# Two hybrid decoder layers on one core: the mixers' small VectorE operations merged or moved to GpSimd and ScalarE

## The chip, the core and the metric

The kernel runs on one core of a Trainium2 chip. The metric is the time of one execution in microseconds of the device, from the start of the program to its end; a kernel is timed several times and the median counts. The profile beside it comes from one further execution. The engines are TensorE (PE in the rows, with its weight loads as PEld), VectorE (DVE), ScalarE (ACT), GpSimd (POOL), and SyncE (SP), which issues the DMAs here.

## What is computed

Two decoder layers over 512 tokens of width 1024, in float32. Each layer is a SwiGLU feed-forward (inner width 2816), a mixer, and a second SwiGLU, each with a residual and a layer norm behind it. The mixer projects the stream once and runs three token mixers side by side: RWKV-7 (8 heads of 64), differential attention with ALiBi (4 heads), and a chunked gated DeltaNet (4 heads of 128). Their outputs go through one projection each, are weighted by sigmoid gates, summed and projected again.

```
for l in range(2):
    x = LN(a*x + 0.5*swiglu(x, ffn1))
    h = x @ mix_w_in                                   # 1024 -> 8456 columns
    ya = rwkv7(h[...])        # l2norm of keys, decay cumulated over 64 tokens, state update, group norm
    yb = diff_attention(h[...])   # softmax(q1 k1) - lam*softmax(q2 k2), rmsnorm
    yc = gated_deltanet(h[...])   # conv, l2norm of q and k, exp(G_i - G_j) inside chunks of 64, rmsnorm
    merged = sum_n sigmoid(h[gates_n]) * (y_n @ w_branch[n])
    x = LN(a*x + merged @ mix_w_out)
    x = LN(a*x + 0.5*swiglu(x, ffn2))
```

## The kernel before

Activations stand with their features on the partitions (`xTh`, `xTl`: 128 x 8 x 512, a rounded part and its remainder). Weights come in by DMA as 128x1024 tiles `wr`; ScalarE rounds each to `wh` and VectorE subtracts to `wl`, and a product is three TensorE passes (high x high, high x low, low x high). `proj` makes one tile of 128 features x 512 tokens in 24 such passes of 512 columns; these are the `pj`, `pg`, `pu` and `pgt` matmuls in the rows.

The feed-forwards are long runs of these. In the mixer (`mix`, `main`) the twelve head units of a layer come in the order `RDRDRRDGGDGG`: R is a pair of RWKV heads (`rw_pair`), D an attention head (`da_head`), G a DeltaNet head (`gdn_head`). `main` is the stream of projections; each unit is a generator that yields between its stages, and up to four units are open. `pump` decides when the next stage of a unit is written into the program: a planner (`Estimate`, lines 81 to 132) adds up a price for every instruction on its engine, and a stage is let in when its inputs are due by the planner's own TensorE time. So the planner's prices set the order in which TensorE meets projections and unit stages, and each engine then works its instructions off in order. The prices are on lines 91 to 95 and 113: 70 ns plus 0.52 or 1.04 ns for each element on VectorE, 80 ns plus an 1/1.2 ns each (94 ns more with a scalar of the tile) on ScalarE, 150 ns plus 2.1 ns each on GpSimd, but 600 ns plus 150 ns for each column of a power.

Places that the change touches:

- `rsqrt` (L258) scales and adds on VectorE, and then makes the inverse root. For one column (the layer norms) that is a power on GpSimd; for 4 or 8 columns it is 11 VectorE operations of 128x4 or 128x8, a bit trick and three Newton steps, in which each needs the one before. `rw_pair` calls it for the group norm (L1005, 8 columns, tile `gn`; then `Y` is scaled and transposed into `pyT`), `gdn_head` for the key and query norms (L1121, 8 columns, `gnrm`) and its output norm (L1211, 4 columns, `gss`), `da_head` for its output norm (L1283, 4 columns, `dss`). That is 32 calls: 16 with 8 columns, 16 with 4. The temporary tiles are `rst` and `rsy`.
- `rw_pair` cumulates the decay `G` by eight scans of 64 tokens (L822), and masks and scales its triangular matrix `L` out of PSUM by eight operations of 128x128 (L879). `L` then goes through `inverse`, which writes it to memory by DMA and reads its 16x16 blocks back as `LX`; 15 rounds of two small VectorE operations (`Tb`, `LX`) invert them.
- `gdn_head` makes, for each half of the tokens, the operands `gr` of the decay matrix by eight 128x128 operations (L1137).
- `da_head` negates a row maximum `dmx` for each of the two maps of a block (L1260) and takes the exponential right behind it (L1261).
- All 128x128 temporaries share 12 buffers (L163).

Of the kernel before, what the change touches and what calls it, by code (L numbers as in the profile page):

```python
# [134 lines left out]
class Net:  # L135
# [17 lines left out]
    def t2(self, shape=(128, 512), dt=F32, name="t2"):  # L153
        return self.t2p.tile(list(shape), dt, tag="t2", name=name)
# [5 lines left out]
        return self.smp.tile([128, n], F32, tag=name, name=name, bufs=bufs)  # L160

    def m128(self, name):
        return self.smp.tile([128, 128], F32, tag="m", name=name, bufs=12)  # L163

    def mm(self, out, lhsT, rhs, **kw):
        return self.nc.tensor.matmul(out, lhsT, rhs, **kw)
# [16 lines left out]
    def more_consts(self):  # L183
        nc, c = self.nc, self.const
        P = 128

        def tri(name, sign, base):
            m = c.tile([P, P], F32, name=name)
            nc.gpsimd.affine_select(out=m, in_=self.ones, pattern=[[-sign, P]], compare_op=ALU.is_ge,
                                    fill=0.0, base=base, channel_multiplier=sign)  # L190
            return m

        self.m_gt = tri("m_gt", 1, -1)
        self.m_le = tri("m_le", -1, 0)
        self.r_gt, self.r_le = (c.tile([P, P], F32R, name=n) for n in ("r_gt", "r_le"))
        nc.gpsimd.tensor_copy(out=self.r_gt, in_=self.m_gt)
        nc.gpsimd.tensor_copy(out=self.r_le, in_=self.m_le)
        self.r_id = c.tile([P, P], F32R, name="r_id")
        nc.gpsimd.tensor_copy(out=self.r_id, in_=self.ident)
        self.neg = c.tile([P, 2, 2, P], F32R, name="neg")  # L200
        for i, m in enumerate((self.m_gt, self.m_le)):
            for j in range(2):
                nc.gpsimd.tensor_scalar(out=self.neg[:, i, j, :], in0=m, scalar1=1e30, scalar2=-1e30, op0=ALU.mult,
                                        op1=ALU.add)

        def pair(name, src, r0):
            m = c.tile([P, P], F32, name=name)
            nc.gpsimd.tensor_copy(out=m, in_=src)
            nc.gpsimd.memset(m[r0:r0 + 64, 64 - r0:128 - r0], 0.0)
            return m  # L210

        self.b_gt = pair("b_gt", self.m_gt, 64)

        self.m3 = c.tile([P, 3, 64], F32, name="m3")
        for h in range(2):
            r = slice(64 * h, 64 * h + 64)
            for j in range(3):
                nc.gpsimd.affine_select(out=self.m3[r, j, :], in_=self.ones[r, 0:64], pattern=[[1, 64]],
                                        compare_op=ALU.is_ge, fill=0.0, base=-1 if j == 0 else 0, channel_multiplier=-1)
        self.bd = c.tile([P, P], F32, name="bd")  # L220
        nc.gpsimd.memset(self.bd, 0.0)
        nc.gpsimd.memset(self.bd[0:64, 0:64], 1.0)
        nc.gpsimd.memset(self.bd[64:128, 64:128], 1.0)
        self.r_bd = c.tile([P, P], F32R, name="r_bd")
        nc.gpsimd.tensor_copy(out=self.r_bd, in_=self.bd)

        b, nb = 16, P // 32
        self.lev = c.tile([P, P], F32, name="lev")
        nc.gpsimd.memset(self.lev, 0.0)
        v = self.lev.rearrange("p (n h b) -> p n h b", h=2, b=b)[:, :, 0, :]  # L230
        nc.gpsimd.memset(v, 1.0)
        nc.gpsimd.affine_select(out=v, in_=v, pattern=[[-2 * b, nb], [0, b]], compare_op=ALU.is_ge,
                                fill=0.0, base=-b, channel_multiplier=1)
        nc.gpsimd.affine_select(out=v, in_=v, pattern=[[2 * b, nb], [0, b]], compare_op=ALU.is_ge,
                                fill=0.0, base=2 * b - 1, channel_multiplier=-1)
        zt = self.t2(name="zt")
        nc.gpsimd.memset(zt, 0.0)
        self.xd, self.nxd = [], 0
        for _ in range(3):
            t = self.tc.dram_tile([8 * BLK], F32, name="Xd")  # L240
            nc.sync.dma_start(out=t[0:128 * 1024].rearrange("(p c) -> p c", p=128)[:, 0:512], in_=zt)
            nc.sync.dma_start(out=t[0:128 * 1024].rearrange("(p c) -> p c", p=128)[:, 512:1024], in_=zt)
            nc.sync.dma_start(out=t[128 * 1024:].rearrange("(p c) -> p c", p=128), in_=zt[:, 0:8])
            self.xd.append(t)

        self.ndist = c.tile([P, 512], F32, name="ndist")
        nc.gpsimd.iota(self.ndist, pattern=[[1, 512]], base=-384, channel_multiplier=-1,
                       allow_small_or_imprecise_dtypes=True)
        nc.gpsimd.affine_select(out=self.ndist, in_=self.ndist, pattern=[[-1, 512]], compare_op=ALU.is_ge,
                                fill=-1e30, base=384, channel_multiplier=1)  # L250
        self.mhalf = c.tile([P, 16], F32, name="mhalf")
        nc.gpsimd.memset(self.mhalf, -0.5)
# [5 lines left out]
    def rsqrt(self, out, in_, scale, eps, n):  # L258
        nc = self.nc
        nc.vector.tensor_scalar(out=out, in0=in_, scalar1=scale, scalar2=eps, op0=ALU.mult, op1=ALU.add)  # L260
        if n == 1:
            nc.gpsimd.tensor_tensor(out=out, in0=out, in1=self.mhalf[:, 0:n], op=ALU.pow)
            return

        V, y, t = nc.vector, self.sm(n, "rsy"), self.sm(n, "rst")
        V.tensor_scalar(out=t.bitcast(I32), in0=out.bitcast(I32), scalar1=1, scalar2=None, op0=ALU.logical_shift_right)
        V.tensor_scalar(out=y.bitcast(I32), in0=t.bitcast(I32), scalar1=-1, scalar2=0x5f3759df, op0=ALU.mult, op1=ALU.add)
        for i in range(3):
            V.tensor_tensor(out=t, in0=y, in1=y, op=ALU.mult)
            V.scalar_tensor_tensor(out=t, in0=t, scalar=-0.5, in1=out, op0=ALU.mult, op1=ALU.mult)  # L270
            V.scalar_tensor_tensor(out=out if i == 2 else y, in0=t, scalar=1.5, in1=y, op0=ALU.add, op1=ALU.mult)

# [521 lines left out]
    def rw_pair(self, j, r, k, v):  # L796
# [22 lines left out]
        sq = t2(name="sq")  # L819
        nc.scalar.activation(out=sq, in_=p.rearrange("p t c -> p (t c)"), func=ACTF.Square)  # L820
        G = t2(name="G")
        for c in range(8):  # L822
            s = slice(64 * c, 64 * c + 64)
            nc.vector.tensor_tensor_scan(out=G[:, s], data0=self.ones[:, 0:64], data1=lw[:, s],
                                         initial=0.0, op0=ALU.mult, op1=ALU.add)

        VU, KB = ([t2((128, 4, 128), name=n) for _ in range(2)] for n in ("VU", "KB"))
        p = self.psum((128, 4, 128), "pv2")
# [32 lines left out]
        for h in range(2):  # L861
            TT(out=c4(AR[h][:, :, 0, :])[:, :, :, 1:64], in0=c4(AR[h][:, :, 0, :])[:, :, :, 1:64],
               in1=c4(hv(E, h))[:, :, :, 0:63], op=ALU.mult)
            nc.gpsimd.tensor_tensor(out=AR[h][:, :, 1, :], in0=hv(r, h), in1=hv(E, h), op=ALU.mult)
        yield

        pb = self.psum(name="pb")
# [2 lines left out]
        bv = v  # L870
        TT(out=bv, in0=v, in1=pb, op=ALU.mult)

        Ls = [t2((128, 4, 128), name="L") for _ in range(2)]
        ps = [self.psum((128, 4, 128), "pL") for _ in range(2)]
        for tt in range(NT):
            for e in range(2):
                rs = slice(64 * e, 64 * e + 64)
                self.mm(ps[e][:, tt, :], AR[tt // 2][rs, tt % 2, 0, :], be[rs, 128 * tt:128 * tt + 128], start=True, stop=True)
        for e in range(2):  # L879
            for tt in range(NT):  # L880
                STT(out=Ls[e][:, tt, :], in0=ps[e][:, tt, :], scalar=n2[:, 2 * tt + e:2 * tt + e + 1], in1=self.b_gt,
                    op0=ALU.mult, op1=ALU.mult)
        yield
        inv = self.inverse([L.rearrange("p a b -> p (a b)") for L in Ls], False)
        next(inv)
# [216 lines left out]
    def gdn_head(self, h, k, q, v, sz):  # L1102
# [30 lines left out]
        for tp in range(2):  # L1133

            gr = [t2((128, 2, 2, 128), dt=F32R, name="gr") for _ in range(2)]
            for e in range(2):
                for q in range(2):  # L1137
                    g1 = self.g2[e][:, 2 * tp + q, h:h + 1]
                    nc.vector.tensor_scalar(out=gr[e][:, 0, q, :], in0=self.m_gt, scalar1=g1, scalar2=None, op0=ALU.mult)
                    nc.vector.tensor_scalar(out=gr[e][:, 1, q, :], in0=self.m_le, scalar1=g1, scalar2=None, op0=ALU.mult)  # L1140
            yield
            pd = self.psum((128, 2, 2, 128), "pd")
            self.mm(pd, self.r_id, self.neg, start=True, stop=False, skip_group_check=True)
            for e in range(2):
                self.mm(pd[:, 0], self.r_le, gr[e][:, 0], start=False, stop=e == 1, skip_group_check=True)
            for e in range(2):
# [92 lines left out]
    def da_head(self, h, q, k, v):  # L1239
# [7 lines left out]
        for i in range(NT):  # L1247
            n = 128 * (i + 1)
            ex = []
            sm = self.sm(2, "dsum", bufs=4)  # L1250
            for m in range(2):
                w = max(n, 256)
                p = self.psum((128, w), "psc")
                self.mm64(p, q, k, m, slice(128 * i, 128 * i + 128), slice(0, w))
                p = p[:, 0:n]
                t = t2((128, n), name="dsc")
                mx = self.sm(2, "dmx", bufs=4)
                nc.vector.tensor_tensor_reduce(out=t, in0=p, in1=self.ndist[:, 128 * (3 - i):512], scale=1.0,
                                               scalar=-3e38, op0=ALU.add, op1=ALU.max, accum_out=mx[:, 0:1])
                nc.vector.tensor_scalar(out=mx[:, 1:2], in0=mx[:, 0:1], scalar1=-slope, scalar2=None, op0=ALU.mult)  # L1260
                nc.scalar.activation(out=t, in_=t, func=ACTF.Exp, scale=slope, bias=mx[:, 1:2], accum_out=sm[:, m:m + 1])  # L1261
                ex.append(t)
            yield

            c = self.sm(2, "dc", bufs=4)
# [159 lines left out]
```

## Time and profile before

| | |
|---|---|
| timed runs | 2860.83, 2865.65, 2866.03 us; median 2865.65 us |
| profiled execution | 2866.84 us, of which the span from its first to its last instruction is 2865.0 us |
| TensorE busy | 2817.8 us (98% of the span), 15728 matmuls |
| VectorE busy | 1657.9 us (58%), 3760 instructions |
| ScalarE busy | 1015.4 us (35%), 1805 instructions |
| GpSimd busy | 157.2 us (5%), 205 instructions |
| the mixers | about 400 to 870 us and 1800 to 2340 us of the span |

Busy means that at least one instruction of the engine was under way; a matmul of 512 columns lasts 389 ns in the record although 222 of them start in 50 us of a feed-forward, so a busy TensorE need not be at its best rate. A wait is idle time of an engine, put down to the instruction that released it. The granted clock is the share of full speed that TensorE was given; it has two levels, 1.2 and 2.4 GHz, shown as 0.50 and 1.00.

### The profile page before, as it was taken

The numbers are of one execution on the slowest core, as the hardware profiler recorded it, in microseconds if no ns is written. First come the engines' busy times: TensorE is split into PE (matmuls) and PEld (weight loads), VectorE is DVE, ScalarE is ACT, GpSimd is POOL, SyncE is SP. The second block draws the span as 40 slices with busy tenths as digits, with TensorE's granted clock in tenths as the row PEclk, the third lists the DMA queues.
The fourth block names the chain that finished last, engine by engine and source line by source line (L and its number), as shares of the span: only waits on it lengthen the run. The fifth ranks groups of instructions, "written<-read, shape, count | busy, mean of one in ns | idle before, by whom it ended". The sixth has DMA issues, their size and how long they took to land. (4 is left out here: it accounts for less than half of the span.)

```text
span 2865.0 us, 40194 instructions
## 1 busy us (share of the span) xinstructions
PE 2817.8 (98%) x15728; PEld 2333.7 (81%) x15728; DVE 1657.9 (58%) x3760; ACT 1015.4 (35%) x1805; POOL 157.2 (5%) x205
## 2 busy tenths in 40 slices
PE   9999999999999999999999999999999999999998
PEld 8888887778878888888888888777788788888887
DVE  4333568788874463443643335677888745633345
ACT  3222345444543332222422223454445433322222
POOL 1000021010000010000100000210100000100001
PEclk9999999999999999999999999999999999999999
DMA  6433423222223353333533334222222234533332
GB/s 179 126 98 99 141 75 84 67 72 55 71 72 88 101 180 101 98 96 97 155 96 113 101 96 134 82 71 69 69 61 65 72 89 117 163 109 97 96 96 89
DMA packets 436350, 282.18 MB, mean 98 GB/s; under 512 B 39432, under 2 KB 391872, under 8 KB 436160
## 3 DMA queue, kind: packets, MB, share of 16 engines
q1 hardware_dynamic: 436160, 279.60, 33.5%
q8 instruction: 124, 2.03, 0.3%
q14 instruction: 66, 0.54, 0.1%
HBM read 258.31 MB, written 21.25 MB: 98 GB/s over the span
## 5 line engine op out<-in xcount | busy, mean ns | idle before, releaser
L66 DVE TENSOR_TENSOR wl<-wr,wh 128x1024 fp32r<-128x1024 f32 x406 | 500.1, 1232 | 655.7 <-ACT wh L66 652.4
L66 ACT CAST wh<-wr 128x1024 fp32r<-128x1024 f32 x406 | 427.4, 1053 | 1252.4 <-issue 550.9
L66 PE MATMUL pu<-xTh,wh 128*128 128x512 f32 x672 | 261.6, 389 | 0.0
L66 PE MATMUL pu<-xTh,wl 128*128 128x512 f32 x672 | 261.4, 389 | 0.0
L66 PE MATMUL pu<-xTl,wh 128*128 128x512 f32 x672 | 261.4, 389 | 0.0
L66 PE MATMUL oa<-wh,hl 128*128 128x512 f32 x640 | 249.0, 389 | 0.0
L66 PE MATMUL pg<-xTh,wh 128*128 128x512 f32 x640 | 249.0, 389 | 0.0
L66 PE MATMUL pg<-xTl,wh 128*128 128x512 f32 x640 | 249.0, 389 | 0.0
L66 PE MATMUL pg<-xTh,wl 128*128 128x512 f32 x640 | 249.0, 389 | 0.0
L66 PE MATMUL oa<-wh,hh 128*128 128x512 f32 x640 | 249.0, 389 | 0.0
L66 PE MATMUL oa<-wl,hh 128*128 128x512 f32 x640 | 249.0, 389 | 0.0
L66 PE MATMUL pj<-xTh,wh 128*128 128x512 f32 x560 | 229.1, 409 | 0.0
L66 PE MATMUL pj<-xTh,wl 128*128 128x512 f32 x560 | 227.7, 407 | 0.0
L66 PE MATMUL pj<-xTl,wh 128*128 128x512 f32 x560 | 225.7, 403 | 0.0
L66 DVE TENSOR_TENSOR ft<-ft,pu 128x512 f32<-128x512 f32 x84 | 57.7, 687 | 226.5 <-PE pu L66 226.4
L66 PE MATMUL pgt<-xTh,wh 128*128 128x512 f32 x384 | 153.0, 398 | 0.0
L66 PE MATMUL pgt<-xTh,wl 128*128 128x512 f32 x384 | 150.4, 392 | 0.0
L66 PE MATMUL pgt<-xTl,wh 128*128 128x512 f32 x384 | 150.3, 391 | 0.0
L66 PEld LDWEIGHTS pu<-xTh,wl 128*128 128x128 f32 x672 | 126.2, 188 | 26.2
L66 PEld LDWEIGHTS pu<-xTl,wh 128*128 128x128 f32 x672 | 126.2, 188 | 26.0
L66 PEld LDWEIGHTS pu<-xTh,wh 128*128 128x128 f32 x672 | 126.0, 188 | 26.2
L66 PEld LDWEIGHTS pg<-xTh,wh 128*128 128x128 f32 x640 | 120.2, 188 | 25.2
(397 smaller groups left out, 5295.5 us busy)
## 6 DMA issues: line engine op xcount, KB each, us to landing
wr<-in_ffn_w_in_dram SPq DMA_DIRECT2D x176, 512.0 KB
wr<-in_mix_w_in_dram SPq DMA_DIRECT2D x132, 512.0 KB
wr<-in_ffn_w_out_dram SPq DMA_DIRECT2D x88, 512.0 KB
wr<-in_mix_w_branch_dram SPq DMA_DIRECT2D x24, 512.0 KB
xres<-x SPq DMA_DIRECT2D x40, 256.0 KB
x<-xres SPq DMA_DIRECT2D x40, 256.0 KB
wr<-in_mix_w_out_dram SPq DMA_DIRECT2D x16, 512.0 KB
iX<-Xd SPq DMA_DIRECT2D x24, 256.0 KB
```

The costliest lines, as they stand in the source:

```text
L66: r = f(*args, **kw)
```

## The change

- `rsqrt` keeps its first VectorE operation and makes the inverse root by one GpSimd power for any number of columns.
- The eight scans become one of 512 columns, with a constant `seg` (ones, but zero at the start of each 64) that multiplies the running sum.
- The eight masked and scaled copies of `L` become eight ScalarE copies of the mask scaled by the norm, made one stage earlier, and two VectorE products of 128x512 with PSUM.
- The eight `gr` operations become two VectorE products of 128x512 with broadcast operands; the constant `neg` is halved and broadcast into its matmul.
- The two negations of `dmx` become one, and both exponentials stand behind both reductions.
- The buffers of the 128x128 temporaries go from 12 to 10.

```diff
     def rsqrt(self, out, in_, scale, eps, n):
         nc.vector.tensor_scalar(out=out, in0=in_, scalar1=scale, scalar2=eps, op0=ALU.mult, op1=ALU.add)
-        if n == 1:
-            nc.gpsimd.tensor_tensor(out=out, in0=out, in1=self.mhalf[:, 0:n], op=ALU.pow)
-            return
-        V, y, t = nc.vector, self.sm(n, "rsy"), self.sm(n, "rst")
-        V.tensor_scalar(out=t.bitcast(I32), in0=out.bitcast(I32), scalar1=1, scalar2=None, op0=ALU.logical_shift_right)
-        V.tensor_scalar(out=y.bitcast(I32), in0=t.bitcast(I32), scalar1=-1, scalar2=0x5f3759df, op0=ALU.mult, op1=ALU.add)
-        for i in range(3):
-            V.tensor_tensor(out=t, in0=y, in1=y, op=ALU.mult)
-            V.scalar_tensor_tensor(out=t, in0=t, scalar=-0.5, in1=out, op0=ALU.mult, op1=ALU.mult)
-            V.scalar_tensor_tensor(out=out if i == 2 else y, in0=t, scalar=1.5, in1=y, op0=ALU.add, op1=ALU.mult)
+        nc.gpsimd.tensor_tensor(out=out, in0=out, in1=self.mhalf[:, 0:n], op=ALU.pow)
...
-        for c in range(8):
-            s = slice(64 * c, 64 * c + 64)
-            nc.vector.tensor_tensor_scan(out=G[:, s], data0=self.ones[:, 0:64], data1=lw[:, s],
-                                         initial=0.0, op0=ALU.mult, op1=ALU.add)
+        nc.vector.tensor_tensor_scan(out=G, data0=self.seg, data1=lw,
+                                     initial=0.0, op0=ALU.mult, op1=ALU.add)
...
+        Ls = [t2((128, 4, 128), name="L") for _ in range(2)]
+        for e in range(2):
+            for tt in range(NT):
+                nc.scalar.activation(out=Ls[e][:, tt, :], in_=self.b_gt, func=ACTF.Copy, scale=n2[:, 2 * tt + e:2 * tt + e + 1])
         yield
...
         for e in range(2):
-            for tt in range(NT):
-                STT(out=Ls[e][:, tt, :], in0=ps[e][:, tt, :], scalar=n2[:, 2 * tt + e:2 * tt + e + 1], in1=self.b_gt,
-                    op0=ALU.mult, op1=ALU.mult)
+            TT(out=Ls[e], in0=ps[e], in1=Ls[e], op=ALU.mult)
...
             for e in range(2):
-                for q in range(2):
-                    g1 = self.g2[e][:, 2 * tp + q, h:h + 1]
-                    nc.vector.tensor_scalar(out=gr[e][:, 0, q, :], in0=self.m_gt, scalar1=g1, scalar2=None, op0=ALU.mult)
-                    nc.vector.tensor_scalar(out=gr[e][:, 1, q, :], in0=self.m_le, scalar1=g1, scalar2=None, op0=ALU.mult)
+                TT(out=gr[e], in0=self.m_2[:, :, None, :].to_broadcast([128, 2, 2, 128]),
+                   in1=self.g2[e][:, None, 2 * tp:2 * tp + 2, h:h + 1].to_broadcast([128, 2, 2, 128]), op=ALU.mult)
...
-                nc.vector.tensor_scalar(out=mx[:, 1:2], in0=mx[:, 0:1], scalar1=-slope, scalar2=None, op0=ALU.mult)
-                nc.scalar.activation(out=t, in_=t, func=ACTF.Exp, scale=slope, bias=mx[:, 1:2], accum_out=sm[:, m:m + 1])
                 ex.append(t)
+            nc.vector.tensor_scalar(out=mx[:, 2:4], in0=mx[:, 0:2], scalar1=-slope, scalar2=None, op0=ALU.mult)
+            for m, t in enumerate(ex):
+                nc.scalar.activation(out=t, in_=t, func=ACTF.Exp, scale=slope, bias=mx[:, 2 + m:3 + m],
+                                     accum_out=sm[:, m:m + 1])
```

## Rows read from the trace of the kernel before

**Rows 1.** The page: busy us of each engine, share of the span, instructions.

```profile
PE 2817.8 (98%) x15728; PEld 2333.7 (81%) x15728; DVE 1657.9 (58%) x3760; ACT 1015.4 (35%) x1805; POOL 157.2 (5%) x205
```

**Rows 2.** Mixers: stretch, length, busy PE, PEld, DVE, ACT, POOL, granted clock, DMA.

```profile
400.00:870.00 470.00, 456.21 (x3427) 369.38 (x3426) 381.99 (x1272) 230.46 (x530) 40.18 (x52) 1.00 0.27 70
1800.00:2340.00 540.00, 527.38 (x3791) 430.90 (x3791) 413.34 (x1336) 251.81 (x568) 41.14 (x55) 0.98 0.26 70
```

**Rows 3.** Waits of PE over the span: releaser, us in total, times, longest.

```profile
PE pyT L66 <- DVE Y L66: 4.5, 2, 2.5
PE ip L66 <- DVE iZ L66: 4.2, 4, 1.4
PE pG L66 <- DVE gg L66: 4.0, 2, 2.0
...
PE pb L66 <- ACT sqh L66: 1.1, 2, 0.5
PE pMV L66 <- DVE M L66: 1.0, 2, 0.5
...
PE pyT L66 <- DVE gO L66: 0.7, 2, 0.3
...
PE pyT L66 <- DVE dO L66: 0.5, 1, 0.5
```

**Rows 4.** Timeline, DVE around 552 us: start, length, instruction, idle before.

```profile
550.20 0.16 DVE L66 TENSOR_SCALAR rst<-dss 128x4 int32<-128x4 int32 x1
552.64 0.17 DVE L66 TENSOR_TENSOR Tb<-LX 64x15 f32<-64x15 f32 x1 [2.28 <-DMA LX<-Ld]
```

**Rows 5.** Timeline, PE, layer 1's longest wait for `Y`.

```profile
556.17 0.63 PE L66 MATMUL pyT<-ident,Y 128*128 128x128 f32 x4 [1.94 <-DVE Y L66]
```

**Rows 6.** Timeline, PE, layer 2's longest wait for `Y`.

```profile
1982.45 0.31 PE L66 MATMUL pyT<-ident,Y 128*128 128x128 f32 x1 [2.52 <-DVE Y L66]
```

**Rows 7.** One stretch at the lower clock, and the sum of all four; columns of rows 2.

```profile
1982.60:1986.00 3.40, 3.40 (x14) 3.01 (x14) 1.97 (x9) 1.21 (x2) 0.00 (x0) 0.50 0.00 0
sum 20.40, PE 20.40 PEld 14.96 DVE 14.77 ACT 6.45 POOL 4.03; mean PE 5.10 PEld 3.74 DVE 3.69 ACT 1.61 POOL 1.01
```

**Rows 8.** Whole span, instructions with `rst` alone: busy DVE, clock, DMA.

```profile
0.00:2865.00 2865.00, 53.15 (x352) 0.99 0.34 98
```

**Rows 9.** Timeline, DVE: first and last of eleven operations of one inverse root.

```profile
713.23 0.13 DVE L66 TENSOR_SCALAR rst<-gn 128x8 int32<-128x8 int32 x1
...
716.21 0.17 DVE L66 SCALAR_TENSOR_TENSOR gn<-rst,rsy 128x8 f32<-128x8 f32 x1
```

**Rows 10.** POOL, power of one column: count, least, median, most ns; first and last start.

```profile
L66 POOL TENSOR_TENSOR lnrs<-lnrs,mhalf x24: 547/550/1527, 359.6 to 2859.6; 128x1 f32<-128x1 f32 x24
```

**Rows 11.** Timeline, DVE and POOL around 1428 us.

```profile
1427.13 1.71 DVE L66 TENSOR_TENSOR wl<-wr,wh 128x1024 fp32r<-128x1024 f32 x1
1427.71 1.53 POOL L66 TENSOR_TENSOR lnrs<-lnrs,mhalf 128x1 f32<-128x1 f32 x1
```

**Rows 12.** DVE groups: shapes, count, busy us, mean ns, idle before.

```profile
L66 DVE TENSOR_TENSOR wl<-wr,wh 128x1024 fp32r<-128x1024 f32 x406 | 500.1, 1232 | 655.7 <-ACT wh L66 652.4 <-ACT ipt L66 1.8 <-DMA Ld<-L 0.2
...
L66 DVE SCALAR_TENSOR_TENSOR L<-pL,n,b_gt 128x128 f32<-128x128 f32 x64 | 18.3, 341 | 0.9 <-PE pL L66 0.9
...
L66 DVE TENSOR_TENSOR_SCAN G<-ones,lw 128x64 f32<-128x64 f32 x64 | 12.5, 269 | 0.4
...
L66 DVE TENSOR_SCALAR dmx<-dmx 128x1 f32<-128x1 f32 x64 | 8.6, 143 | 0.1
...
L66 DVE TENSOR_TENSOR R<-pMV,nn 128x512 f32<-128x512 f32 x8 | 5.5, 686 | 1.6 <-PE pMV L66 1.5
```

**Rows 13.** Whole span, instructions with `gr` alone: busy PE, PEld, DVE, clock, DMA.

```profile
0.00:2865.00 2865.00, 11.09 (x64) 9.81 (x64) 29.80 (x128) 0.99 0.34 98
```

**Rows 14.** ACT group: a 128x128 activation with a scalar of the tile.

```profile
L66 ACT ACTIVATE dO<-pdo,drs 128x128 f32<-128x128 f32 x32 | 11.9, 370 | 19.5 <-PE pdo L66 19.3
```

**Rows 15.** Timeline, ACT, the rounding that the `pb` matmul waits for.

```profile
476.00 0.62 ACT L66 CAST sqh<-sq 128x512 fp32r<-128x512 f32 x1 [1.41 <-DVE sq L66]
```

More of the change, by code (lines that the diff above doesn't have):

```diff
@@ L162, in m128 @@
     def m128(self, name):
-        return self.smp.tile([128, 128], F32, tag="m", name=name, bufs=12)
+        return self.smp.tile([128, 128], F32, tag="m", name=name, bufs=10)
     def mm(self, out, lhsT, rhs, **kw):
@@ L185, in more_consts, with tri @@
         P = 128
-        def tri(name, sign, base):
-            m = c.tile([P, P], F32, name=name)
+        self.m_2 = c.tile([P, 2, P], F32, name="m_2")
+        def tri(m, sign, base):
             nc.gpsimd.affine_select(out=m, in_=self.ones, pattern=[[-sign, P]], compare_op=ALU.is_ge,
@@ L191, in tri @@
             return m
-        self.m_gt = tri("m_gt", 1, -1)
-        self.m_le = tri("m_le", -1, 0)
+        self.m_gt = tri(self.m_2[:, 0, :], 1, -1)
+        self.m_le = tri(self.m_2[:, 1, :], -1, 0)
         self.r_gt, self.r_le = (c.tile([P, P], F32R, name=n) for n in ("r_gt", "r_le"))
@@ L199, in more_consts @@
         nc.gpsimd.tensor_copy(out=self.r_id, in_=self.ident)
-        self.neg = c.tile([P, 2, 2, P], F32R, name="neg")
+        self.neg = c.tile([P, 2, P], F32R, name="neg")
         for i, m in enumerate((self.m_gt, self.m_le)):
-            for j in range(2):
-                nc.gpsimd.tensor_scalar(out=self.neg[:, i, j, :], in0=m, scalar1=1e30, scalar2=-1e30, op0=ALU.mult,
-                                        op1=ALU.add)
+            nc.gpsimd.tensor_scalar(out=self.neg[:, i, :], in0=m, scalar1=1e30, scalar2=-1e30, op0=ALU.mult, op1=ALU.add)
         def pair(name, src, r0):
@@ L219, in more_consts @@
                                         compare_op=ALU.is_ge, fill=0.0, base=-1 if j == 0 else 0, channel_multiplier=-1)
+        self.seg = c.tile([P, T], F32, name="seg")
+        nc.gpsimd.memset(self.seg, 1.0)
+        nc.gpsimd.memset(self.seg.rearrange("p (c i) -> p c i", c=8)[:, :, 0:1], 0.0)
         self.bd = c.tile([P, P], F32, name="bd")
@@ L871, in rw_pair @@
         TT(out=bv, in0=v, in1=pb, op=ALU.mult)
-        Ls = [t2((128, 4, 128), name="L") for _ in range(2)]
         ps = [self.psum((128, 4, 128), "pL") for _ in range(2)]
@@ L1136, in gdn_head @@
             for e in range(2):
-                for q in range(2):
-                    g1 = self.g2[e][:, 2 * tp + q, h:h + 1]
-                    nc.vector.tensor_scalar(out=gr[e][:, 0, q, :], in0=self.m_gt, scalar1=g1, scalar2=None, op0=ALU.mult)
-                    nc.vector.tensor_scalar(out=gr[e][:, 1, q, :], in0=self.m_le, scalar1=g1, scalar2=None, op0=ALU.mult)
+                TT(out=gr[e], in0=self.m_2[:, :, None, :].to_broadcast([128, 2, 2, 128]),
+                   in1=self.g2[e][:, None, 2 * tp:2 * tp + 2, h:h + 1].to_broadcast([128, 2, 2, 128]), op=ALU.mult)
             yield
             pd = self.psum((128, 2, 2, 128), "pd")
-            self.mm(pd, self.r_id, self.neg, start=True, stop=False, skip_group_check=True)
+            self.mm(pd, self.r_id, self.neg[:, :, None, :].to_broadcast([128, 2, 2, 128]), start=True, stop=False,
+                    skip_group_check=True)
             for e in range(2):
@@ L1250, in da_head @@
             sm = self.sm(2, "dsum", bufs=4)
+            mx = self.sm(4, "dmx", bufs=4)
             for m in range(2):
@@ L1256, in da_head @@
                 t = t2((128, n), name="dsc")
-                mx = self.sm(2, "dmx", bufs=4)
                 nc.vector.tensor_tensor_reduce(out=t, in0=p, in1=self.ndist[:, 128 * (3 - i):512], scale=1.0,
-                                               scalar=-3e38, op0=ALU.add, op1=ALU.max, accum_out=mx[:, 0:1])
-                nc.vector.tensor_scalar(out=mx[:, 1:2], in0=mx[:, 0:1], scalar1=-slope, scalar2=None, op0=ALU.mult)
-                nc.scalar.activation(out=t, in_=t, func=ACTF.Exp, scale=slope, bias=mx[:, 1:2], accum_out=sm[:, m:m + 1])
+                                               scalar=-3e38, op0=ALU.add, op1=ALU.max, accum_out=mx[:, m:m + 1])
                 ex.append(t)
+            nc.vector.tensor_scalar(out=mx[:, 2:4], in0=mx[:, 0:2], scalar1=-slope, scalar2=None, op0=ALU.mult)
+            for m, t in enumerate(ex):
+                nc.scalar.activation(out=t, in_=t, func=ACTF.Exp, scale=slope, bias=mx[:, 2 + m:3 + m],
+                                     accum_out=sm[:, m:m + 1])
             yield
```

## The prediction

> **What bounds the kernel now.** The first part of the page comes first: TensorE is busy for 2817.8 of 2865.0 us, VectorE for 1657.9 [rows 1]. So 47.2 us is all that better timing can give without less matmul work, and the change takes away no matmul. The table by stretches says where to look: in the two mixers TensorE idles for 13.8 us (470.0 - 456.21) and 12.6 us (540.0 - 527.38), 26.4 us together, while VectorE is busy for 81% and 77% [rows 2]. The feed-forwards and their layer norms hold the other 20.8 us, and nothing in them changes: their one-column roots are powers already. Then the waits of TensorE: nearly all those of the mixers end on VectorE [rows 3]. The longest kind is the transpose `pyT` behind the group norm, 4.5 us in two waits. The timeline shows how it comes about: at 550.20 VectorE has made the first step of two inverse roots; the next instruction in its order belongs to the block inversion and waits 2.28 us for a DMA, and the ten steps of each root that are left come behind it, woven among the inversion's small products [rows 4]. TensorE has meanwhile stopped for 1.94 us [rows 5]; layer 2 does the same with 2.52 us [rows 6]. One more loss hangs on such stops: in layer 2's mixer the granted clock is at 0.50 (1.2 GHz) for four stretches, 20.4 us, and one of them, 3.4 us, begins at 1982.6 right behind the 2.52 us stop [rows 6, 7]. Layer 1 has the same stops and no such stretch (clock 1.00 [rows 2]), so a stop makes one possible, not certain.
>
> The profiled execution took 2866.84 us, 1.2 above the median of 2865.65; the sum below starts from 2866.84.
>
> **Inverse roots.** 32 calls lose 11 operations each, 352, which keep VectorE busy for 53.15 us [rows 8]; part of that lies over neighbours, so it is an upper figure. What counts more is the length of the chain: 713.23 to 716.38, 3.15 us, with one weight subtraction in between [rows 9], and from 550.20 past 555 where it waits for the DMA. The power that replaces it is on another engine, whose queue holds 81.3 us of work in both mixers' 1010 us [rows 2], and so cannot be caught behind that DMA wait. Its price for 4 or 8 columns stands in no row. One column takes 550 ns [rows 10]; below, all columns cost what one does, 0.55 us; above, each costs as much, 2.2 and 4.4 us. I take 1.2 and 1.8 us, the planner's own prices and nearer the lower end, since the one-column time must hold a start-up. With 1.8 the chain is shorter than the shortest one measured, and even 4.4 us is under the 5 us around 552.
>
> Contention is the point to be careful about. At 1427.71 a one-column power took 1.53 us beside a VectorE subtraction that took 1.71 [rows 11], against 0.55 and a mean of 1.23 [rows 10, 12]. So up to 1.0 us comes on top of a power, and up to 0.5 us on a VectorE operation; 32 x 0.5 = 16 us of VectorE at most.
> The Trainium skill (GPSIMD Engine Reference, section 8, Key points) says that GpSimd shares its SBUF interfaces with VectorE and contends with operations that have two SBUF inputs; that speaks against this move, and the 1.53 us agrees with it. By that rule the contention would fall on most of the 32 powers; it has its place below as the slow power.
>
> Behind the roots in the program: `Y` is scaled by VectorE in a stage of its own, so other work can stand between; in `gdn_head` (`bs`, `kws`, `nqs`) and before the scaling of `dO` and `gO` the next VectorE operation of the same stage needs the power, and if nothing stands between them VectorE idles for about as long as it worked before. There I count nothing.
>
> So: the two waits for `Y` go, 4.5 us; the wait for `dO` (the chain of its root fills the time ahead of it) 0.5; the two of `pMV` for `M`, in which steps of a root stand between, 1.0 [rows 3]. That is 6.0 us. What is late next behind `Y` is its own scaling, which needs VectorE after the DMA wait, so by 552.64 + 0.67 = 553.3; the stop begins at 556.17 - 1.94 = 554.2, so nothing is left.
>
> **The merged operations.** None stands on a path that TensorE was seen to wait for; they lighten VectorE. `gr`: 29.8 us [rows 13] against 32 products of 128x512 at 0.686 us, 22.0 [rows 12]: 7.8 back.
> The Trainium skill (VectorE: DVE Perf Modes, section The perf-mode tier table) has it the other way: a float32 tensor_scalar in SBUF at twice the rate of a tensor_tensor. By rate alone this merge would cost VectorE time, an estimate of 0.53 us for each of 16 sets from its 0.96 GHz, 8.5 us instead of the gain, and 1.5 us of relief below instead of 1.9. The rows differ from it, and they decide: the fixed part of a 128-column operation outweighs the rate.
> `L`: 18.3 against 16 x 0.686 = 11.0 [rows 12]: 7.3 back. The scans: 12.5 for 64 [rows 12]; one of 512 lies between a product's 0.69 us and eight scans' 1.57; half way, 1.1, gives 3.7 back, the ends 0 and 7. `dmx`: half of 8.6, 4.3 back. With the roots, 76 us of the 795 that VectorE is busy in the mixers [rows 2], 10%. The ten other kinds of wait that end on VectorE there, from `ip` (4.2) by `pG` (4.0) down to `pyT` for `gO` (0.7), make 18.7 us [rows 3]; a tenth of that is 1.9 us. It could be nothing, as most of them end chains that the change leaves alone, or half.
>
> **Added to ScalarE.** 64 copies of 128x128 with a scalar. The nearest row has 0.370 us [rows 14]: 23.7 us, 2.96 for each pair of RWKV heads. ScalarE is busy for 48% of the mixers [rows 2], and it idled 1.41 us before it rounded `sqh`, for which TensorE waits already [rows 3, 15]. The planner adds 2.25 us to that stage and lets the next in later, with projections in between, so I take nothing on TensorE; without cover it is 23.7 us. The rest (two buffers less, one constant read by broadcast) I take at nothing, as no wait in rows 3 is for such a buffer; if one came up, it would cost what a wait there costs, 0.3 to 2.5 us.
>
> **Sum.** 6.0 + 1.9, and the 3.4 us at half clock behind the stop of 1982, half of which is loss, 1.7: 9.6 us. 2866.84 - 9.6 = 2857.2. Against the median that is 8.4 us less, 0.3%.
>
> **Rivals.**
> (a) The gain is taken back by the new order. Prices fall on VectorE and rise on GpSimd and ScalarE, so projections and stages meet in another order everywhere in the mixers, and other waits of half a microsecond to two come up. For it: 26.4 us of waits are left to be dealt anew; against it: the planner prices the eleven operations at 74 to 78 ns, 0.85 us, and they took 3.15 [rows 9], and it is these that go, so that the plan comes nearer to what happens. About 2864 us.
> (b) The other three stretches at half clock go too, (20.4 - 3.4) / 2 = 8.5 us more [rows 7]: 2848.7. For it: layer 1 does without them. Against it: the stops before them (`pG`, `pb`) are not on the changed chains.
> (c) Slower: ScalarE, in order, does the eight copies ahead of `sqh` and of the weights' rounding. Of 2.96 us, 1.41 has cover; 1.55 x 8 = 12.4 us late: 2866.84 - 9.6 + 12.4 = 2869.6. With no cover 2866.84 - 9.6 + 23.7 = 2880.9. It decides from 9.6 / 8 = 1.2 us for each pair that reach TensorE.
> (d) The slow power: 4.4 us and 1.0 for contention, 5.4. The other six pairs show no wait for `Y` [rows 3], with chains 2.3 us over the planned 0.85 [rows 9]; over the power's planned 1.8 that makes 4.1, and 16 x 1.3 = 20.8 us: 2878.0. It decides from 4.7 us for 8 columns.
>
> **Chances.** Forecast 0.42, its own range 2853 to 2861; (a) 0.28; (b) 0.15; (c) 0.10, half of it without cover; (d) 0.05. About 0.2%, 5.7 us, is what a measurement can tell here: below 2859.9 is faster, above 2871.4 slower. Faster: 0.36 of the forecast and 0.15 of (b), 0.51. Slower: 0.05 of (c), 0.05 of (d) and 0.02 of (a), 0.12. Same: 0.37. The range goes from just under (b), 2847, to just over the covered (c), 2870.
>
> **What the changed profile would show.** Right: no `pyT` wait for `Y` over 1 us; powers of 8 columns near 1.8 us; VectorE's busy time down by 50 to 76 us; TensorE idle in the mixers near 18 us. Wrong: waits of TensorE on ScalarE for `sqh` or on `L`; powers over 4 us with VectorE idle behind them; TensorE idle at 26 us again under other names; more stretches at 0.50, which would hide the gain.

## The result, and the profile after

The changed kernel takes 2892.09 us (median of four runs, 2890.37 to 2892.33) against 2865.84 us for the kernel before on the same chip: 1.009 times as long, 95% interval 1.0073 to 1.0108. That is 26 us slower, where 8.4 us less was forecast. Its profiled execution took 2890.37 us with a span of 2888.4 us, 23.4 us more than before.

The page's first part (columns as in [rows 1]) and the mixers by windows (columns as in [rows 2]):

```profile
PE 2828.9 (98%) x15728; PEld 2341.2 (81%) x15728; DVE 1618.5 (56%) x3176; ACT 1030.8 (36%) x1869; POOL 202.8 (7%) x237
```

```profile
400.00:870.00 470.00, 450.79 (x3305) 363.58 (x3304) 352.30 (x959) 230.77 (x545) 60.05 (x66) 0.97 0.26 69
1800.00:2340.00 540.00, 518.17 (x3763) 422.24 (x3762) 398.24 (x1054) 259.36 (x601) 73.58 (x78) 0.99 0.26 69
```

VectorE is busy for 39.4 us less, as the change intends. TensorE nevertheless idles for 19.2 and 21.8 us in the mixers, 41.0 together against 26.4 [rows 2]: 14.6 us more. The clock has fallen as well: the stretches of the changed kernel's mixers at the lower level, by windows:

```profile
430.10:440.34 10.24, 9.85 (x34) 7.48 (x35) 4.09 (x10) 2.75 (x7) 2.15 (x2) 0.50 0.33 89
498.37:508.61 10.24, 10.24 (x80) 7.42 (x81) 5.71 (x22) 1.79 (x4) 0.00 (x0) 0.50 0.20 54
563.22:566.63 3.41, 3.41 (x12) 2.90 (x11) 3.41 (x7) 0.00 (x0) 0.75 (x2) 0.50 0.02 5
...
sum 40.96, PE 40.57 PEld 30.43 DVE 22.17 ACT 7.89 POOL 2.90; mean PE 6.76 PEld 5.07 DVE 3.69 ACT 1.32 POOL 0.48
```

Six stretches, 41.0 us, against four with 20.4 [rows 7]; as 0.50 is half of full speed, half of the 20.6 us more is an estimate of the loss, 10.3 us. 14.6 + 10.3 = 24.9 us is near the 23.4.

Which waits grew: TensorE's over the span (releaser, total, times, longest), to be set against [rows 3].

```profile
PE ip L66 <- DVE iZ L66: 7.0, 8, 1.4
PE pyT L66 <- DVE dO L66: 6.3, 4, 2.2
PE pG L66 <- DVE gg L66: 6.2, 2, 3.1
...
PE pyT L66 <- DVE gO L66: 4.7, 4, 2.1
PE pb L66 <- DVE sql L66: 3.0, 2, 1.5
...
PE pMV L66 <- DVE M L66: 0.6, 2, 0.3
```

The wait for `Y` is gone, as forecast. `dO` (0.5 before) and `gO` (0.7) together have 11.0 us: both are scalings that need a power. VectorE's own waits behind GpSimd say part of why (for `dO` the smaller part, as e13 shows below); before, the only ones were those for the one-column `lnrs`:

```profile
DVE bs L66 <- POOL gnrm L66: 10.4, 6, 1.7
DVE gss L66 <- POOL gss L66: 8.6, 8, 1.1
DVE Y L66 <- POOL gn L66: 7.1, 4, 1.8
DVE dO L66 <- POOL dss L66: 5.2, 8, 0.9
```

VectorE stands still for 31.3 us, in 26 waits behind the 32 powers. At the median the powers are no slower than I priced them, though single ones took up to 2.7 us (count, then least, median, most ns, first and last start; columns as in [rows 10]):

```profile
L66 POOL TENSOR_TENSOR dss<-dss,mhalf x8: 1007/1200/1377, 494.6 to 2233.1; 128x4 f32<-128x4 f32 x8
L66 POOL TENSOR_TENSOR gn<-gn,mhalf x8: 1635/1641/2681, 558.2 to 2172.8; 128x8 f32<-128x8 f32 x8
L66 POOL TENSOR_TENSOR gnrm<-gnrm,mhalf x8: 1635/1636/2562, 659.7 to 2249.6; 128x8 f32<-128x8 f32 x8
L66 POOL TENSOR_TENSOR gss<-gss,mhalf x8: 1006/1007/1007, 770.8 to 2342.7; 128x4 f32<-128x4 f32 x8
```

VectorE's and TensorE's timeline around 560 us shows how such a stop comes about:

```profile
557.08 1.08 DVE L66 TENSOR_SCALAR gn<-gn 128x8 f32<-128x8 f32 x1
559.91 0.69 DVE L66 TENSOR_TENSOR Y<-Y,gn 128x512 f32<-128x512 f32 x1 [1.76 <-POOL gn L66]
...
561.19 0.68 DVE L66 TENSOR_TENSOR sql<-sq,sqh 128x512 fp32r<-128x512 f32 x1
561.93 0.50 PE L66 MATMUL pb<-sql,r_bd 128*128 128x512 f32 x1 [1.50 <-DVE sql L66]
```

`Y` comes next in VectorE's order, its power is not there yet, and VectorE stands for 1.76 us. `sql`, which needs no power at all, stands behind it, and TensorE stops for 1.50 us on `sql`. A half-clock stretch follows at 563.22. The wait is booked under `sql`: the name of a wait is that of the instruction TensorE needs, and the cause stands three instructions ahead of it in VectorE's order.

The merged operations did what was forecast or nearly: `gr` 20.8 us (29.8 [rows 13]), and these VectorE groups (count, busy, mean ns, idle before):

```profile
L66 DVE TENSOR_TENSOR L<-pL,L 128x512 f32<-128x512 f32 x16 | 10.3, 682 | 0.4 <-PE pL L66 0.4
L66 DVE TENSOR_TENSOR_SCAN G<-seg,lw 128x512 f32<-128x512 f32 x8 | 9.8, 1225 | 0.3
L66 DVE TENSOR_SCALAR dmx<-dmx 128x2 f32<-128x2 f32 x32 | 5.5, 172 | 0.6
```

### The profile page after: what moved, and what is told of

It is laid out like the page before. It is cut to its first block, busy times and chain, and to the rows that moved or that the text cites. A ratio compares the mean times of both kernels' runs of the same rounds, so it can differ in the third digit from the quotient of the medians.

```text
span 2888.4 us, 39669 instructions
## 1 busy us (share of the span) xinstructions
PE 2828.9 (98%) x15728; PEld 2341.2 (81%) x15728; DVE 1618.5 (56%) x3176; ACT 1030.8 (36%) x1869; POOL 202.8 (7%) x237
## 5 line engine op out<-in xcount | busy, mean ns | idle before, releaser
L66 PEld LDWEIGHTS pg<-xTh,wl 128*128 128x128 f32 x640 | 120.1, 188 | 25.2
```

The lines of the kernel that those rows point to most:

```text
L66: r = f(*args, **kw)
```

## The experiments

The kernels of one group ran on one chip, beside the kernel before; the ratio is to that. Three columns are worked out from each trace's rows, over both mixers from their first projections to the last `pgt` (395.8 to 1016.1 us and 1817.5 to 2444.6 us in the kernel before; these limits follow the kernel, and the idle times differ by up to 1.4 us from those of the fixed windows shown): TensorE's idle time, its time at half clock, and VectorE's idle time behind GpSimd. They describe one execution of each kernel, and the time at half clock is not the same in all: over its timed runs the kernel before has a mean granted clock of 0.993 to 0.998. For e9 and e15 that execution took 2869.07 and 2860.71 us, well under their medians.

| kernel | median us | ratio, 95% interval | TensorE idle | half clock | VectorE behind GpSimd |
|---|---|---|---|---|---|
| before | 2865.84 | 1 | 26.7 | 20.5 | 0 |
| after | 2892.09 | 1.0090 [1.0073, 1.0108] | 39.6 | 41.0 | 31.3 |
| e1 | 2885.93 | 1.0082 [1.0067, 1.0097] | 34.9 | 30.7 | 0 |
| e2 | 2892.93 | 1.0103 [1.0088, 1.0118] | 39.3 | 41.0 | 28.3 |
| e3 | 2903.76 | 1.0142 [1.0125, 1.0159] | 48.4 | 51.2 | 34.0 |
| e4 | 2887.48 | 1.0085 [1.0070, 1.0100] | 35.8 | 27.3 | 0 |
| e5 | 2871.93 | 1.0027 [1.0010, 1.0045] | 30.4 | 17.1 | 0 |
| e6 | 2863.05 | 0.9996 [0.9985, 1.0007] | 25.8 | 10.2 | 0 |
| e7 | 2939.02 | 1.0255 [1.0212, 1.0299] | 67.3 | 92.2 | 32.6 |
| e8 | 2889.95 | 1.0090 [1.0067, 1.0113] | 41.9 | 41.0 | 31.2 |
| e9 | 2874.98 | 1.0039 [1.0028, 1.0050] | 26.0 | 30.7 | 0 |
| e10 | 2867.56 | 1.0019 [1.0007, 1.0030] | 27.5 | 13.7 | 0 |
| e11 | 2865.66 | 1.0010 [0.9998, 1.0021] | 27.6 | 10.2 | 0 |
| e12 | 2878.25 | 1.0047 [1.0017, 1.0077] | 31.9 | 27.3 | 0 |
| e13 | 2870.44 | 1.0015 [1.0004, 1.0027] | 25.3 | 34.1 | 5.6 |
| e14 | 2862.73 | 0.9988 [0.9977, 1.0000] | 24.5 | 13.7 | 4.6 |
| e15 | 2868.25 | 1.0009 [0.9995, 1.0023] | 25.7 | 6.8 | 0 |
| e16 | 2869.84 | 1.0016 [1.0004, 1.0027] | 29.1 | 20.5 | 7.0 |
| e17 | 2878.46 | 1.0049 [1.0037, 1.0060] | 32.6 | 41.0 | 3.2 |
| e18 | 2885.41 | 1.0072 [1.0057, 1.0087] | 40.0 | 41.0 | 3.1 |

Theory A: VectorE works in order, stands still behind a power whose consumer comes next, and delays what is behind it. Theory B: it is the new order of the stages, whatever the operations take.

**The powers taken out or put in, and the order swapped.** e1 is the changed kernel with the old roots, e2 the old one with the powers alone:

```diff
     # e2, on the kernel before (e1: the reverse, on the changed kernel)
-        if n == 1:
             nc.gpsimd.tensor_tensor(out=out, in0=out, in1=self.mhalf[:, 0:n], op=ALU.pow)
-            return
-        V, y, t = nc.vector, self.sm(n, "rsy"), self.sm(n, "rst")
...
```

In e3 the changed kernel lets its stages in at the moments that the kernel before chose, and e4 the other way round:

```diff
-        it = next((it for it in self.active if it[2] <= self.est.pe.t), None)
...
+        it = self.active[int((self.recf if force else self.step).popleft())]
```

> The changed kernel with its 4- and 8-column inverse roots back on VectorE, everything else as changed. Theory A (VectorE works in order and stands still behind the GpSimd powers; other work that TensorE needs queues behind): near the kernel before or a little under it, 2855 to 2868 us, no TensorE wait over 2 us for dO or gO. Theory B (the planner's new prices deal a worse order of TensorE's stages, whoever works them): undecided, since this variant gets an order of its own, 2860 to 2890. Theory C (the ScalarE masks or the merged products cost the time): about 2890 us still.

> The kernel before with only the inverse roots of 4 and 8 columns moved to GpSimd powers. Theory A: most of the loss, 2880 to 2895 us, with VectorE idle for some 30 us behind powers outside the layer norms. Theory B: an order of its own, 2860 to 2890. Theory C: no loss, 2858 to 2868 us.

> The changed kernel with the unit stages let in exactly in the order in which the kernel before lets them in (the choices of pump written down and replayed), so that the planner's new prices move nothing. Theory A: the loss stays, 2880 to 2895 us, VectorE idle behind powers as long as in the changed kernel. Theory B: the loss is gone, 2855 to 2868 us. Theory C: the loss stays, with waits on ScalarE.

> The kernel before, all its instructions, with the unit stages let in in the order in which the changed kernel lets them in. Theory A: near the kernel before, 2860 to 2872 us. Theory B: as slow as the changed kernel, 2880 to 2895 us. Theory C: near the kernel before.

The powers alone cost 30 us (e2), more than the whole change. But taking them out gives back only 2 us by the ratios, 6 by the medians (e1), and the old operations in the new order cost 24 (e4): order costs too. The old order makes the change worse still (e3). Theory A had e1 and e4 near the kernel before, and theory B had e3 there; none of the three came out so. Both theories live, and both e1 and e2 changed the order with the operation, so that neither settles it. The swapped orders come near the ones that they take without being the same: in e4 13696 of TensorE's 15728 matmuls write the same tile at the same place as in the changed kernel, in e3 13812 as in the kernel before, against 11184 between those two kernels.

**How much a small shift of the order moves.** e5 and e6 are the kernel before, e7 and e8 the changed one, with another price for a change of engines in the planner:

```diff
-    WAIT = 120.0
+    WAIT = 110.0   # e5, e7; 130.0 in e6, e8
```

> The kernel before with the planner's allowance for a hand-over between engines at 110 ns for 120: no instruction changes, only the order in which stages are let in. Theory D (the order of the kernel before happens to suit its instructions, and most other orders cost 15 to 30 us, with more stops of TensorE and more time at half clock): 2875 to 2895 us. Theory A (what costs is what the changed instructions do): 2858 to 2870 us.

> The same with 130 ns, which moves fewer instructions than 110 does. Theory D: between the kernel before and 2890 us. Theory A: 2858 to 2870 us.

> The changed kernel with the allowance at 110 ns. Theory D: another draw, anywhere from 2865 to 2900 us, on average like the variants of the kernel before. Theory A: 2885 to 2900 us, over each variant of the kernel before by 20 us or more.

> The changed kernel with the allowance at 130 ns. Theory D: another draw, 2865 to 2900 us. Theory A: 2885 to 2900 us.

The kernel before moves by -3 to +6 us; the changed one stays at +24 to +26 or gets far worse. In e7 one wait makes 17.8 of the 27.7 us by which TensorE idles more than in the changed kernel (total, times, longest):

```profile
PE pj L66 <- DVE dq L66: 17.8, 2, 8.9
```

So among these four neighbours the 26 us are no unlucky draw, but an order can cost more than the change. e5 lies between the ranges of theories A and D.

**The parts alone.** Each of the other edits on the kernel before, as in the diff of the change: the masks on ScalarE (e9), `gr` (e10), the scan (e11, with the 10 buffers and the halved `neg`), `dmx` (e12).

> The kernel before with only the masked scales of L moved to ScalarE and the two products of 128x512. Theory E (the merged and moved operations other than the powers cost their 20 us by one of them that turns the order of TensorE's stages over; this one moves few instructions): 2860 to 2870 us. Theory C (the ScalarE copies stand ahead of sqh and of the weights' rounding): 2875 to 2885 us.

> The kernel before with only the merged products gr and the halved constant neg. Theory E: 2860 to 2875 us, as its order differs by half as much as that of the changed kernel. Theory F (each edit costs its share by itself): about 5 us over the kernel before.

> The kernel before with only the one scan with resets (and neg halved and broadcast, without which it does not fit the memory). Theory E: 2860 to 2870 us, few instructions move. Theory F: about 5 us over.

> The kernel before with only the merged negation in the attention heads, which puts both exponentials behind both reductions. Theory E: this is the one; it moves as many of TensorE's instructions as the whole change does: 2875 to 2890 us. Theory F: about 5 us over.

`gr` costs 5 us, the scan 3 (its interval includes none), the masks 12, `dmx` 15, the powers 30: 65 us apart, 26 together. The parts don't add. In e12 `dmx` became cheaper by itself (8.6 to 5.4 us), and these waits, which the kernel before does not have, came up elsewhere:

```profile
PE pkk L66 <- ACT AR L66: 4.9, 2, 2.5
...
PE pz L66 <- DVE cv L66: 2.8, 2, 1.4
```

The first stands in e4 with the same 4.9 us and without a changed instruction, so that it belongs to the order. e9 came out at the lower edge of theory C's range, and not in that of theory E.

**The power's length alone, every order kept.** What was missing is a run in which only a duration changes. e13 (the changed kernel) and e14 (e2) put a product of the same shape on GpSimd in the power's place; the planner still prices it as a power, so every engine's instructions stand in the same order; the traces of e13 and the changed kernel, and of e14 and e2, show it for TensorE, VectorE, ScalarE and GpSimd. The line with the planner's price is left out here:

```diff
-        nc.vector.tensor_scalar(out=out, in0=in_, scalar1=scale, scalar2=eps, op0=ALU.mult, op1=ALU.add)
-        nc.gpsimd.tensor_tensor(out=out, in0=out, in1=self.mhalf[:, 0:n], op=ALU.pow)
+        nc.vector.tensor_scalar(out=out, in0=in_, scalar1=scale * (1e-6 if n > 1 else 1), scalar2=eps, op0=ALU.mult, op1=ALU.add)
+        nc.gpsimd.tensor_tensor(out=out, in0=out, in1=self.mhalf[:, 0:n], op=ALU.mult if n > 1 else ALU.pow)
```

e15 is the kernel before with 32 powers more, which nobody waits for:

```diff
+        z = self.smp.tile([128, 16], F32, tag="dead", name="dead", bufs=2)[:, 0:n]
+        nc.vector.eng.tensor_scalar(out=z, in0=out, scalar1=1.0, scalar2=None, op0=ALU.mult)
+        nc.gpsimd.eng.tensor_tensor(out=z, in0=z, in1=self.mhalf[:, 0:n], op=ALU.pow)
```

> The changed kernel, each engine's instructions in exactly the same order, but the 4- and 8-column power is a multiplication by the same constant, planned at the price of a power: the inverse root itself is left out. Theory A (VectorE and the stages wait for the power's length): VectorE's 31 us behind powers fall under 10, and the time to 2865 to 2880 us. Theory B (the order alone costs): 2886 to 2895 us still.

> The same shortening in the kernel before with only the powers moved (2893 us with real powers): the inverse root is left out here too. Theory A: 2863 to 2875 us. Theory B: 2886 to 2895 us.

> The kernel before with its roots on VectorE and beside each of the 32 a GpSimd power of the same size on a copy, not known to the planner, whose result nobody waits for. Theory A: 2863 to 2872 us. Theory G (a power costs by its contention with VectorE and by holding up GpSimd's queue): 2878 us or more.

This decides how much hangs on the power's length. The GpSimd operations and VectorE's waits for them in e13 (views as above):

```profile
L66 POOL TENSOR_TENSOR gn<-gn,mhalf x8: 202/204/1232, 558.5 to 2156.7; 128x8 f32<-128x8 f32 x8
```

```profile
DVE gss L66 <- POOL gss L66: 1.9, 6, 0.3
DVE bs L66 <- POOL gnrm L66: 1.8, 6, 0.3
DVE Y L66 <- POOL gn L66: 1.4, 4, 0.4
```

and the mixers of e13:

```profile
400.00:870.00 470.00, 457.28 (x3385) 369.97 (x3385) 360.04 (x974) 235.03 (x556) 43.48 (x66) 0.98 0.26 69
1800.00:2340.00 540.00, 525.99 (x3807) 430.50 (x3806) 400.24 (x1055) 260.40 (x604) 49.42 (x75) 0.99 0.27 71
```

With 1.4 us less in an eight-column operation TensorE's idle time is 26.7 us in these windows (12.7 + 14.0), near the 26.4 before, and about 21 of the 26 us are gone; of the powers alone, all 30. The dead powers, as long as the real ones (0.999 to 2.547 us), most likely cost 2.5 us, with an interval from -0.05 to +0.23%, 6.6 us: neither GpSimd's time nor contention is the price of the 26 us, but that something waits for the power. The stop at `sql` shows it. In e13 `Y` waits for 0.32 us, and TensorE meets `sql` without a stop:

```profile
558.74 0.69 DVE L66 TENSOR_TENSOR Y<-Y,gn 128x512 f32<-128x512 f32 x1 [0.32 <-POOL gn L66]
...
560.02 0.69 DVE L66 TENSOR_TENSOR sql<-sq,sqh 128x512 fp32r<-128x512 f32 x1
560.76 0.49 PE L66 MATMUL pb<-sql,r_bd 128*128 128x512 f32 x1
```

What e13 does not separate is how a power holds TensorE up: through what stands behind its consumer, as `sql` does, or through the consumer itself, as with `gO` (4.7 us, 2.5 in e13).

Not all that grew hangs on the power. The stop at `dO`, 6.3 us in the changed kernel, is still 5.1 us in e13, booked there under `Tb`:

```profile
PE pyT L66 <- DVE Tb L66: 5.1, 2, 2.5
```

There VectorE stood behind the power for only 0.53 us; what else makes the stop, the order or the GpSimd product beside `dO` (last section), was not separated. The half-clock stretches behind this stop and behind the 3.1 us stop for `gg` stay as well: 34.1 us in e13, of the changed kernel's 41.0.

**Other work between power and consumer.** e16 is the changed kernel in which the stage yields behind the power, and the consumer is bound behind the VectorE work that was written in between. e17 does that with the powers alone, e18 with the powers, `gr` and the scan.

```diff
         self.rsqrt(nrm, nrm, 1.0, 4e-6, 8)
+        yield
+        self.est.vector.inorder = True
...
         TT(out=bs, in0=nrm[:, 0:4], in1=self.beta[:, :, h], op=ALU.mult)
...
+        self.est.vector.inorder = False
```

> The changed kernel with a stage boundary between each power and what needs it, and the consumer bound behind the VectorE work that was let in in between. Theory A: VectorE's idle time behind powers falls from 31 us to under 12, and the time to 2870 to 2882 us. Theory B: another draw of the order, 2875 to 2900 us, whatever the idle time does.

> The kernel before with the 4- and 8-column powers alone, their consumers bound behind VectorE work that does not need them. Theory A (VectorE standing still behind a power, with the stops that follow, is the price of the powers): 2858 to 2868 us against 2892.93 for the powers with their consumers in place, and VectorE's idle time behind GpSimd under 8 us in the mixers. Rival (each new order is a draw of its own, and the idle time only goes with it): 2865 to 2885 us with VectorE's idle time behind GpSimd under 8 us all the same.

> The same with the one-step gr and the one scan beside the powers; without the masks on ScalarE and the one-step dmx. Theory A: 2858 to 2870 us, since what is left of the change stands on no chain that ends a stop of TensorE; a version that beats the kernel before by more than 0.2% would need the half-clock stretches to go as well (20.5 us in the mixers before). Rival (each order is a draw): anywhere from 2860 to 2885 us, as gr alone (2867.56) and the scan alone (2865.66) do not add to the powers' figure.

In e16 the powers are as they were (1.0 us for 4 columns and 1.6 for 8 at the least), and about 21 us come back. VectorE and GpSimd in e16, where the changed kernel stood for 1.76 us:

```profile
550.18 1.08 DVE L66 TENSOR_SCALAR gn<-gn 128x8 f32<-128x8 f32 x1
551.18 1.21 DVE L66 TENSOR_TENSOR wl<-wr,wh 128x1024 fp32r<-128x1024 f32 x1
552.32 0.68 DVE L66 TENSOR_TENSOR R<-pMV,nn 128x512 f32<-128x512 f32 x1
...
552.99 0.68 DVE L66 TENSOR_TENSOR sql<-sq,sqh 128x512 fp32r<-128x512 f32 x1
...
557.71 1.41 DVE L66 TENSOR_TENSOR Y<-Y,gn 128x512 f32<-128x512 f32 x1
```

```profile
551.35 2.55 POOL L66 TENSOR_TENSOR gn<-gn,mhalf 128x8 f32<-128x8 f32 x1
```

`sql` now stands ahead of `Y`, and 2.55 us of power are hidden. But e16 has an order of its own too, and e17 and e18 went as the rival expected (e18 at the edge of its range): VectorE stands for 3.2 us in all, and they are 14 and 21 us slower than before. Their largest new wait in e17:

```profile
PE pgw L66 <- DVE rk L66: 5.5, 2, 2.7
```

```profile
786.97 0.28 DVE L66 TENSOR_SCALAR gr<-m_gt,gh 128x128 fp32r<-128x128 f32 x1
...
788.73 0.28 DVE L66 TENSOR_SCALAR rk<-Kt,kws 128x128 f32<-128x128 f32 x1
```

The work let in ahead of the consumer, eight `gr` operations here, makes `rk`, a product with `kws` from the root, late for TensorE; a half-clock stretch of 10.2 us begins at 789.39. Binding the consumer behind other work therefore trades one wait for another, and which is dearer is a matter of the order. No version beats the kernel before by more than a measurement can tell.

## Why the prediction was wrong

**The step that failed** is the sentence on `gdn_head`, `dO` and `gO`: "if nothing stands between them VectorE idles for about as long as it worked before. There I count nothing." The observation was right and its price was not nothing. While VectorE made the root itself, the planner could write other VectorE work among the eleven steps, and did ([rows 9]: a weight subtraction within the chain). Behind a power in another queue, what is written next on VectorE is mostly the consumer, and everything behind it waits. That is 31 us of VectorE's time. TensorE idles for 12.9 us more, and the clock costs an estimated 10.2 us. With nothing but the power shortened (e13) about 21 of the 26 us come back: all of the idle time, and 3.4 us of the clock's; e16 gives back as much. The other 6.8 us of the clock's stay in e13, behind the stops for `gg` and `dO`, and are not the power's, as far as one execution of each kernel shows.

**"`Y` is scaled by VectorE in a stage of its own, so other work can stand between"** was wrong for half of its eight cases: four waits of up to 1.8 us, and the one at 559.91 stops TensorE.

**The waits to be removed.** `pyT` behind `Y`, 4.5 us: gone, as forecast. `pMV`: 1.0 to 0.6. `dO`: not 0.5 less but 5.8 more, of which the power's length makes 1.2 (6.3 against 5.1 in e13).

**The price of a power**, taken as 1.2 and 1.8 us, was 1.0 and 1.64 undisturbed and 2.68 at most. Rival (d) put the slow side at 5.4 us, deciding from 4.7, and asked whether the chain gets longer. The chain did get shorter: from the first operation of a root to its consumer it took 7.6 us before and 1.5 after for `dss`, 5.4 and 1.9 for `gnrm`, 4.2 and 1.3 for `gss` (medians of eight). What got longer is VectorE's standing. The sign "powers over 4 us with VectorE idle behind them" had the idle time, and tied it to a length that no power had.

**The relief of VectorE.** `gr` 9.0 us back (7.8 forecast), `L` 8.0 (7.3), the scan 2.7 (3.7), `dmx` 3.1 (4.3). All of VectorE is 39.4 us less busy, not 76: the four give 22.8, so that 16.6 are left for the 53.15 us of `rst`, the rest of which lay over neighbours or went into slower operations (not separated). No gain of TensorE's from it can be seen: a tenth of 18.7 us was forecast, and the wait of `ip` for `iZ` alone grew by 2.8, while `pd` now waits 2.2 us for the merged `gr`.
On `gr` the rates in the Trainium skill (VectorE: DVE Perf Modes, section The perf-mode tier table), taken alone, would have had the merge lose time; with 20.8 us against 29.8 this trace does not agree for operations of 128 columns.

**The ScalarE copies** (rival c): 20.3 us as 64 of 392 ns, and TensorE's wait for `sqh` fell from 1.1 to 0.4. So the late `sqh` did not come. What makes the 12 us of the masks alone (e9) is open: its trace has 10.2 us more at half clock and no more idle time, but that execution took 5.9 us less than the median, and in it TensorE waits 2.8 us for `sql` (0.9 before), which needs `sqh`. That could be the order or the copies.

**The new order** (rival a) was priced as a gain taken back, to 2864. e4, which changes no instruction, shows that an order alone can cost 24 us; e1, e12, e17 and e18, which change some and stand behind GpSimd for 3.2 us at most, are 13 to 24 us slower. The kernel before is near the best of the orders tried: of twelve other kernels without long standing (e1, e4 to e6, e9 to e12, e14, e16 to e18) none is faster by over 0.2%. I took its 26.4 us of waits as something to be dealt anew without a sign, where an order this good makes worse likelier than better.

**The clock**: one stretch was to go (1.7 us gained). It went, but 20.5 us more came than went, 13.6 of which e13 keeps. That stops make such stretches possible was right, with the sign the other way.

**What stays open**: why each single order costs what it does. In e4 the idle time and half of the time at half clock make only 12.5 of the 20.4 us by which its span is longer. e13 leaves a span 3.8 us longer than before with less idle time (25.3 against 26.7) and 13.6 us more at half clock, half of which is 6.8; its first stretch follows the 3.1 us wait for `gg`, which is in the changed kernel with or without powers (e1, e13, e16 have it, e2 has 2.0). The masks alone (e9, 3.0) and the scan alone (e11, 2.7) lengthen that wait; `gr` and `dmx` alone leave it at 2.0 (e10, e12). By which instructions they do it was not followed.

## What to carry to other kernels

Moving a step to an idle engine can cost more than it saves if the busy engine's next instruction in order is the consumer: price the round trip as idle time of the in-order engine, plus whatever stands behind the consumer, and read who that is from the timeline. To find what a changed operation costs, change its duration and keep every order (leave the planner's price); undoing an edit redraws the order and can hide it. And where few orders are better than the one at hand, expect an edit that moves the planner's prices to cost something before it gains.

## What the runs showed of the hardware that was not expected

A GpSimd product of 128x512 can stretch a small VectorE operation that runs beside it. The changed kernel's timeline of VectorE and GpSimd, where GpSimd's next product starts as the power's end releases the consumer:

```profile
494.56 1.02 POOL L66 TENSOR_TENSOR dss<-dss,mhalf 128x4 f32<-128x4 f32 x1 [15.16 <-DVE dss L66]
495.56 2.47 POOL L66 TENSOR_TENSOR imL<-L,lev 128x512 f32<-128x512 f32 x2
495.62 1.28 DVE L66 TENSOR_SCALAR dO<-dO,dss 128x128 f32<-128x128 f32 x1 [0.53 <-POOL dss L66]
496.82 1.27 DVE L66 TENSOR_TENSOR Tb<-LX 64x39 f32<-64x39 f32 x1
498.01 0.27 DVE L66 TENSOR_SCALAR dO<-dO,dss 128x128 f32<-128x128 f32 x1
498.21 0.18 DVE L66 TENSOR_TENSOR LX<-LX,Tb 64x39 f32<-64x39 f32 x1
```

The same `dO` takes 1.28 us beside `imL` and 0.27 us behind it, and a product of 64x39 takes 1.27 where the next takes 0.18. The Trainium skill (GPSIMD Engine Reference, section 8, Key points) says that GpSimd contends with VectorE operations that have two SBUF inputs or run in a 2-port mode. The trace agrees for the 64x39 product, which has two inputs; in which mode `dO` ran, with its one tensor operand, no run shows. In e13, with the short operation, the collision is there all the same, and it is not what separates the changed kernel from e13:

```profile
496.99 1.33 DVE L66 TENSOR_SCALAR dO<-dO,dss 128x128 f32<-128x128 f32 x1
```

A stop is not paid once: in the mixers of the two kernels stretches at 0.50 of 3.4, 6.8 or 10.2 us followed stops of 1.5 to 3.1 us, or two stops of 0.5, and the changed kernel's 20.5 us more of them make an estimated 10.2 of the 23 us. The length of a stretch does not go by that of the stop: behind the stop for `gg`, 3.1 us in both layers of the changed kernel, it was 10.2 us in layer 1 and 3.4 in layer 2.
